# Soft routing over eight experts: five pairs of the first outer product in front, and in four of them a third splitting of inner products 1 and 5

## The chip, the cores and the metric

The kernel runs on one core of one Trainium2 chip. Five engines work side by side, each through its own list of instructions and in order: TensorE (PE, matrix multiplies into the eight banks of PSUM), VectorE (DVE), ScalarE (ACT), GpSimd (POOL, which here mostly issues transfers) and SyncE (SP, which issues transfers). Semaphores order them against each other. The metric is the device time in microseconds; smaller is better. What is compared is the median of several runs.

## The reference

```python
logits_max = np.max(router_logits, axis=-1, keepdims=True)
probs = np.exp(router_logits - logits_max)
probs = probs / np.sum(probs, axis=-1, keepdims=True)
for e in range(n_experts):
    expert_out = np.matmul(x, expert_weights[e])
    output += probs[:, :, e:e+1] * expert_out
```

x has 16 x 512 = 8192 rows (tokens) of 512, there are 8 experts with weights of 512 x 2048, and the output has 8192 x 2048. Since the probability of an expert scales a row, the sum over experts is one product: for a token, the eight scaled copies of its row lie side by side (4096 long) and are multiplied by the eight weight matrices stacked on each other (4096 x 2048).

## The kernel before

**Two levels of seven products.** That large product is cut by the method of Strassen in Winograd's form, which makes a 2 x 2 block product out of seven block products and some sums instead of eight. The outer level halves the experts (0 to 3, 4 to 7) and the output columns, and pairs two blocks of 256 tokens. Its seven products have the numbers r = 1 to 7, and each is taken for 16 values of q, one for each pair of token blocks. `product(r, q)` (L615 of the kernel before) sets one up; such a pair (r, q) is called an instance here. An instance multiplies a left operand of 256 tokens by 2048 (four experts of 512) with a right operand of 2048 x 1024.

The inner level cuts an instance again into seven. The left operand has two tiles `t[0]` and `t[1]` (two experts each), every one with eight chunks of 128 in the contraction and 256 tokens. Class `Left` (L426) makes them on VectorE (`times`, x times probability, 128x2048), and makes from them the difference `s2` (128x1024) and the differences `i` (128x2048). The right operands w[1] to w[7] are tiles of eight chunks by 512 columns; some are weight blocks as they were cast, others are differences that VectorE makes (128x4096). One inner product is eight matmuls, each with 128 x 128 stationary values from the left operand and 512 moving columns. So an instance is 7 x 8 matmuls.

**Steps and banks.** The inner products are taken in the order `STEPS = (1, 5, 6, 2, 7, 3, 4)`. `Product.step` (L498) issues the matmuls. Steps 1, 6, 7 and 4 go on accumulating in one PSUM bank x; steps 5 and 3 use a bank q; step 2 adds onto a bank b. `Product.post` (L506) then evacuates the partial sum: for an instance without a base, ScalarE copies x to b after step 1 (L519), copies q and x into SBUF tiles after steps 5 and 6 (L523), copies after steps 2 and 4 (L527), and VectorE adds after steps 7 and 3. For an instance that continues on an earlier result (a base), VectorE adds at nearly all steps (`post_on_base`). Every finished 128x512 piece is sent to HBM by POOL: the first outer product goes to a buffer `kept`, others to the output.

**Pools.** One PSUM pool has eight buffers, which are the eight banks. In SBUF, tag w has 15 buffers (weights, 128x4096), z has 8 (left operands), h has 12 (pieces of 128x512), and d has 3 (`s2`).

**Stages.** `add` collects one or two instances in a stage; there are 15 of them up to r = 5. A stage with two takes the steps of both alternately, 14 slots in all. `run` (L685) goes through the slots; after each it lets VectorE do other work (`slack`) and evacuates. Hooks placed with `at(stage, slot, ...)` start weight casts, fetches of kept pieces and sums at a slot. The first stages are four pairs of r = 1 (q = 2 to 9), then six stages that hold r = 2 for q = 9 to 14 beside r = 1 for q + 1, whose result passes from the one to the other on chip, and then five pairs of r = 2. The weights for r = 2 are cast in stages 0 to 2 and summed in stage 3. `wedge_at` makes weights of later outer products in stages 4 to 9.

**What orders the work.** A planner in the program keeps two clocks, `clock["pe"]` and `clock["dve"]`. Sums for VectorE wait in `queue` with a planned cost. `slack` advances TensorE's clock by one step (`SLOT`, 1.73) and takes tasks from the queue while VectorE's clock is more than `LAG` behind it; `evacuated` charges an evacuation to VectorE. The resulting order is fixed when the kernel is built. Each engine follows it strictly.

**The head.** Instances r = 1, q = 0 and 1 are computed directly, before the stages. TensorE scales x by diagonal matrices (`early_z0`), and then for each half n of the columns adds 64 matmuls of 512 columns into four banks (the loop `for n in range(2)`). After each n ScalarE copies the four banks out (L331). Meanwhile VectorE and ScalarE work out the softmax of all tokens (`softmax_of_all`, casts at L296 and L297), and for n = 1 TensorE also transposes x for the next two instances (`early_xp1`).

In the listing `ps` is any PSUM tile, `mm` (L127 in the rows of the profile) issues a matmul, and `tt` (L107) issues a VectorE operation on two tensors.

Of the kernel before, what the change touches and what calls it, by code (L numbers as in the profile page):

```python
# [31 lines left out]
def kernel(  # L32
# [51 lines left out]
    with tc.tile_pool(name="psum0", bufs=1, space=bass.MemoryType.PSUM) as psum0:  # L84
# [21 lines left out]
    def tt(o, a, b, op):  # L106
        dve(nc.vector.tensor_tensor(out=o, in0=a, in1=b, op=op))  # L107
# [14 lines left out]

    def bank():
        return psum.tile([P, NB], f32, name="ps", tag="ps")

    def mm(ps, z, w, start, stop):
        note(nc.tensor.matmul(ps, z, w, start=start, stop=stop, skip_group_check=True))  # L127
# [3 lines left out]
    def new_w():  # L131
        return wpool.tile([P, K8, NB], f16, name="w", tag="w")
# [31 lines left out]
    def inner_sums(b, t7=None):  # L164

        w = {1: b[0, 0], 2: b[1, 0], 3: b[1, 1], 7: t7 or b[0, 1]}

        def step(p, x, y):
            if p not in w:
                w[p] = new_w()  # L170
            tt(w[p], x, y, SUB)
        return w, {5: lambda: step(5, b[0, 1], b[0, 0]), 6: lambda: step(6, b[1, 1], w[5]),
                   4: lambda: step(4, b[1, 0], w[6]), 7: lambda: step(7, b[1, 1], b[0, 1])}

    def softmax(lg, J, pf):
        mx = h_tile([P, J], f32)
# [71 lines left out]

    def early_z0(e, d):
        for j in range(4):  # L250
            ps = bank()
# [10 lines left out]

    def early_xp1(j, d):
        t, rows = j // 2 - 2, ds(j % 2 * P, P)
        ps = bank()
# [3 lines left out]
        ps = bank()  # L269
# [38 lines left out]
    for n in range(2):  # L308
        ps = [bank() for _ in range(4)]
        for e in range(HE):  # L310
            if n == 0 and e < 2:
                early_z0(e + 2, ds_[e + 2])
                if e == 0:
                    ds_.append(diag_e(3))
            if n == 0 and e == 2:
                ph0.append(early_p(1))
                ds_ = [diag_j(j) for j in range(4, 8)]
                softmax_of_all()
                w, sums = inner_sums(b11, new_w())
            for c in range(C):  # L320
                for j in range(4):
                    mm(ps[j], z0[j][:, e, c], b11[e // 2, n][:, e % 2 * C + c, :],
                       e + c == 0, e == HE - 1 and c == C - 1)
            if n == 1:
                for j in ((4, 5), (6, 7), (), ())[e]:
                    early_xp1(j, ds_[j - 4])
                if e == 1:
                    sums[5]()
        for j in range(4):
            o = half()  # L330
            act(nc.scalar.copy(o, ps[j]))  # L331
            sp(kept[j // 2][n].rearrange("(p j) m -> j p m", j=2)[j % 2], o)
# [31 lines left out]
        (queue.appendleft if first else queue.append)(t)  # L364
        return t

    def slack():
        clock["dve"] = max(clock["dve"], clock["pe"])
        clock["pe"] += SLOT
        while queue and clock["dve"] < clock["pe"] - LAG:  # L370
            queue.popleft().run()

    def evacuated():
        clock["dve"] = max(clock["dve"], clock["pe"]) + 0.69


    x_dram = {}
# [48 lines left out]
    class Left:  # L426
# [36 lines left out]
        def op(self, p):  # L463
# [4 lines left out]
                    3: (self.i, 0), 7: (self.i, 1)}[p]  # L468
            return t[:, :, ds(i * HP, HP)]

    class Right:


# [16 lines left out]
    class Product:  # L490
# [41 lines left out]
        def post_on_base(self, p, x, q, b):  # L532
# [13 lines left out]
            else:  # L546
                tt(o[tn], q if p in (5, 3) else x, base, ADD)


    def out_rows(q, odd, cols, tn):  # L550
        t, n = tn
# [24 lines left out]
    def at(stage, slot, make):  # L576
        hooks.setdefault((stage, slot), []).append(make)
# [37 lines left out]
    def product(r, q, **how):  # L615
        left, loads = left_of(r, q)
        lefts[r, q] = left
        p = None
        if r == 1:
            def sink(tn, o):  # L620
                pool(kept_rows(q)(tn), o)
            p = Product(right[1], left, sink)
        elif r == 2:
            if q >= 9:
# [24 lines left out]
        products[r, q] = p  # L649
        return p  # L650
# [23 lines left out]
    def queue_left(left):  # L674
        if not left.task:
            left.queue_make(0)
            left.queue_s2()
            left.queue_make(1)

    def queue_lefts(stage):  # L680
        if stage < len(stages):
            for p in stages[stage]:
                queue_left(p.left)

    def run(stage):  # L685
        some = stages[stage]
        for p in some:
            p.left.queue_i()
        n = 0
        for i in range(len(some[0].steps)):  # L690
            for p in some:
                for make in hooks.get((stage, n), ()):
                    make()
                p.step(p.steps[i])
                slack()
                p.post(p.steps[i])
                n += 1
                if n == 1:
                    queue_lefts(stage + 1)
                if n == late.get(stage, 1):  # L700
                    start_loads(stage + 2)
                if n == 5:
                    store_loads(stage + 1)
                if n == 7:
                    finish_loads(stage + 2)
# [10 lines left out]
    forget(*range(0, 18, 2))  # L716
    rest = [15] + list(range(9))
    for i in range(0, 10, 2):
        k = add(product(2, rest[i]), product(2, rest[i + 1]))
        for slot, tn in zip((8, 10, 12, 13), INNER):  # L720
            for q in rest[i:i + 2]:
                if q < 9:
# [83 lines left out]
    def cast21(kn):  # L806
        b21[kn] = cast_block(21, kn)

    for i, kn in enumerate(((0, 0), (0, 1), (1, 1), (1, 0))):
        at((11 * i + 8) // 14, (11 * i + 8) % 14, lambda kn=kn: cast21(kn))  # L810

    def sums_at(stage, slot, r, of, ps):
        def go():
            if right[r].w is None:
                right[r].sums = right[r].build(of)
            for p in ps:
                right[r].queue_sum(right[r].sums, p)
        at(stage, slot, go)
    sums_at(3, 3, 2, b21, (5,))
    sums_at(3, 5, 2, b21, (6,))  # L820
    sums_at(3, 7, 2, b21, (7,))
    sums_at(3, 12, 2, b21, (4,))
# [224 lines left out]
```

## Time and profile before

| what | value |
|---|---|
| median of three runs | 1375.59 us (1375.47 to 1375.77) |
| the profiled execution's own time | 1376.63 us |
| its span | 1374.9 us |
| TensorE busy | 1367.3 us, 99% of the span |
| VectorE busy | 1108.6 us, 81% |
| ScalarE busy | 183.1 us, 13% |
| POOL busy | 411.8 us, 30% |
| DMA read and written | 207.65 MB and 156.43 MB in HBM |

The profile is of one execution. Its times start with the span, and what lies around the span is the difference to the execution's own time. A row of instructions names the line, engine, operation and tiles (out<-in), the shapes, the count, the busy time with the mean length of one, and the idle time of the engine before these instructions with what ended it. In the timeline, a row is a start, a length, the engine and its instructions merged. Matmuls overlap in the pipeline: a row's length runs from the first start to the last end, and the mean length of one is longer than the distance between two starts. A line such as L107 or L127 is a helper through which most instructions of that engine go, so tiles and shapes tell them apart.

### The profile page before, as it was taken

The numbers are of one execution on the slowest core, as the hardware profiler recorded it, in microseconds if no ns is written. First come the engines' busy times: TensorE is split into PE (matmuls) and PEld (weight loads), VectorE is DVE, ScalarE is ACT, GpSimd is POOL, SyncE is SP. The second block draws the span as 40 slices with busy tenths as digits, with TensorE's granted clock in tenths as the row PEclk, the third lists the DMA queues.
The fourth block names the chain that finished last, engine by engine and source line by source line (L and its number), as shares of the span: only waits on it lengthen the run. The fifth ranks groups of instructions, "written<-read, shape, count | busy, mean of one in ns | idle before, by whom it ended". The sixth has DMA issues, their size and how long they took to land.

```text
span 1374.9 us, 17480 instructions
## 1 busy us (share of the span) xinstructions
PE 1367.3 (99%) x6390; PEld 622.0 (45%) x6390; DVE 1108.6 (81%) x1290; ACT 183.1 (13%) x317; POOL 411.8 (30%) x652
## 2 busy tenths in 40 slices
PE   8999999999999999999999999999999999999998
PEld 4444444444444444444444444444444444444444
DVE  5846757669889888798897988889889898988882
ACT  3222111100011111111111100000000000222221
POOL 3222333241223342334232122242333322232221
PEclk9999999999999999999999999999999999999999
DMA  9998999999898998899898998988898979987786
GB/s 183 222 261 205 211 248 265 241 299 378 240 323 249 285 300 246 259 261 265 245 276 263 338 392 219 224 236 212 229 237 223 247 204 316 249 187 177 166 150 106
DMA packets 191271, 338.02 MB, mean 246 GB/s; under 512 B 52944, under 2 KB 86992, under 8 KB 187472
## 3 DMA queue, kind: packets, MB, share of 16 engines
q0 software_dynamic: 88688, 185.12, 55.8%
q1 hardware_dynamic: 98464, 123.34, 30.8%
q10 hardware_dynamic: 4032, 28.44, 5.3%
q8 instruction: 50, 0.82, 0.2%
q14 instruction: 37, 0.30, 0.1%
HBM read 207.65 MB, written 156.43 MB: 265 GB/s over the span
## 4 chain that ended last, share of the span: by engine, by line
PE 98%; DMA 2%; POOL 0%; issue 0%; ACT 0%; POOLq 0%
PE ps L127 98%; DMA w<-wd 1%; DMA w<-in_expert_weights_dram 1%; POOL w L121 0%; ACT h L999 0%; POOL ident L211 0%; POOLq L211 0%; POOLq L1031 0%
## 5 line engine op out<-in xcount | busy, mean ns | idle before, releaser
L127 PE MATMUL ps<-w,z 128*128 128x512 f16 x5416 | 1177.3, 379 | 1.3 <-DMA w<-in_expert_weights_dram 1.1
L127 PEld LDWEIGHTS <-z 128*128 128x128 f16 x5416 | 529.7, 98 | 638.6 <-DMA w<-in_expert_weights_dram 1.3
L121 POOL DMA_DIRECT2D out_dram<-h x380 | 248.9, 672 | 746.4 <-ACT h L540 373.7
L107 DVE TENSOR_TENSOR h<-ps,h 128x512 f32<-128x512 f32 x415 | 282.5, 687 | 207.6 <-PE ps L127 192.8
L107 DVE TENSOR_TENSOR z<-xT,pT 128x2048 f16<-128x2048 f16 x220 | 266.8, 1216 | 11.5 <-DMA xT<-xs 6.3
L127 PE MATMUL ps<-w,d 128*128 128x512 f16 x880 | 199.1, 379 | 0.0
L127 PEld LDWEIGHTS <-d 128*128 128x128 f16 x880 | 86.1, 98 | 103.8
L107 DVE TENSOR_TENSOR z<-z,d 128x2048 f16<-128x2048 f16 x110 | 132.1, 1215 | 0.0
L107 DVE TENSOR_TENSOR w<-w 128x1024 f16<-128x1024 f16 (+2 forms) x92 | 100.8, 1102 | 5.1 <-DMA wd<-w 3.4
L527 ACT COPY h<-ps 128x512 f32<-128x512 f32 x90 | 52.8, 586 | 373.4 <-PE ps L127 336.3
L540 ACT COPY h<-ps 128x512 f32<-128x512 f32 x64 | 37.5, 587 | 486.3 <-PE ps L127 459.9
L107 DVE TENSOR_TENSOR d<-z 128x1024 f16<-128x1024 f16 x110 | 75.2, 685 | 6.8 <-PE ps L127 5.0
L107 DVE TENSOR_TENSOR z<-z,u 128x2048 f16<-128x2048 f16 x64 | 78.4, 1225 | 2.2
L107 DVE TENSOR_TENSOR u<-xT,pT 128x2048 f16<-128x2048 f16 x64 | 77.9, 1217 | 0.0
L523 ACT COPY h<-ps 128x512 f32<-128x512 f32 x90 | 52.8, 587 | 173.9 <-PE ps L127 162.5
L121 POOL DMA_DIRECT2D w<-in_expert_weights_dram x65 | 49.0, 785 | 33.8 <-DMA wd<-w 24.0
L121 POOL DMA_DIRECT2D wd<-w x86 | 48.3, 585 | 36.0 <-DVE w L107 26.4
L107 DVE TENSOR_TENSOR ps<-ps,h 128x512 f32<-128x512 f32 (+1 forms) x66 | 45.3, 688 | 13.0 <-PE ps L127 13.0
L121 POOL DMA_DIRECT2D kept<-h x56 | 30.8, 551 | 76.8 <-ACT h L527 48.2
L107 DVE TENSOR_TENSOR h<-h 128x512 f32<-128x512 f32 (+2 forms) x69 | 45.1, 674 | 0.1
L519 ACT COPY ps<-ps 128x512 f32<-128x512 f32 x45 | 25.6, 570 | 114.6 <-PE ps L127 114.6
L107 DVE TENSOR_TENSOR z<-z 128x2048 f16<-128x2048 f16 x32 | 39.2, 1225 | 1.1
(47 smaller groups left out, 97.0 us busy)
## 6 DMA issues: line engine op xcount, KB each, us to landing
out_dram<-h POOLq DMA_DIRECT2D x380, 256.0 KB, 6.2
pT<-p_dram SPq DMA_DIRECT2D x140, 256.0 KB, 6.0
w<-wd ACTq DMA_DIRECT2D x27, 1024.0 KB, 9.9
h<-kept SPq DMA_DIRECT2D x100, 256.0 KB, 5.6
xT<-x SPq DMA_DIRECT2D x87, 256.0 KB, 5.5
wd<-w POOLq DMA_DIRECT2D x72, 256.0 KB, 5.5
w<-in_expert_weights_dram POOLq DMA_DIRECT2D x35, 512.0 KB, 10.1
h<-out_dram SPq DMA_DIRECT2D x68, 256.0 KB, 5.6
```

The source lines that it names most:

```text
L107: dve(nc.vector.tensor_tensor(out=o, in0=a, in1=b, op=op))
L121: note(nc.gpsimd.dma_start(out=o, in_=i, **how))
L127: note(nc.tensor.matmul(ps, z, w, start=start, stop=stop, skip_group_check=True))
L519: act(nc.scalar.copy(self.banks["b"], x))
L523: act(nc.scalar.copy(o[tn], q if p == 5 else x))
L527: act(nc.scalar.copy(o[TN[p]], b if p == 2 else x))
L540: act(nc.scalar.copy(o[tn], b))
```

## The change

The stages in front become five pairs of r = 1 (q = 2 to 11; `QK = 11`), then four stages with r = 2 for q = 11 to 14 beside r = 1 for q + 1, and six pairs of r = 2. The number of stages stays 15. Casts and sums of weights and the wedges move to stages up to one later (`ND = QK // 2`). Instances 9 and 10 of r = 2 now fetch their base from `kept`.

In stages 1 to 4, the inner products 1 and 5 of both instances of the pair are split a third time. The left block matrix of that level has the two instances as its rows and the two halves of `t[0]` (experts) as its columns; the right one is w[1] or w[5], cut into 4 chunks each way by 256 columns. Each of the two products becomes seven short steps of four matmuls with 256 columns. `third_sums` makes the right differences once, in the head, into two more w tiles; class `Thirds` makes four left sums (128x1024) a stage into h tiles. `by_thirds` issues the 14 short steps in a fixed order, with one x bank for each of the products 1 and 5, one q bank shared by both, and four banks g and h that collect the sums, which the rest of the stage then uses as its x and q. Evacuations in between are copies of 256 columns on ScalarE and adds of 256 columns on VectorE.

The PSUM pool is divided: six buffers for tag ps and two for tag pt. The q bank of ordinary stages, the two x banks of `by_thirds`, and every second bank of `early_z0` and `early_xp1` in the head come from pt.

```diff
-    psum = ctx.enter_context(tc.tile_pool(name="psum", bufs=8, space=bass.MemoryType.PSUM))
+    psum = ctx.enter_context(tc.tile_pool(name="psum", bufs=6, space=bass.MemoryType.PSUM))
...
+    def bank2():
+        return psum.tile([P, NB], f32, name="pt", tag="pt", bufs=2)
...
+    def third_sums(w):
+
+        t = new_w().rearrange("p (s c) (h n) -> p s c h n", s=2, h=2)
+        t = {5: t[:, 0, :, 0], 6: t[:, 0, :, 1], 7: t[:, 1, :, 0], 4: t[:, 1, :, 1]}
+        b = w.rearrange("p (k c) (h n) -> p k c h n", k=2, h=2)
+        tt(t[5], b[:, 0, :, 1], b[:, 0, :, 0], SUB)
+        tt(t[6], b[:, 1, :, 1], t[5], SUB)
+        tt(t[7], b[:, 1, :, 1], b[:, 0, :, 1], SUB)
+        tt(t[4], b[:, 1, :, 0], t[6], SUB)
+        return {**t, 1: b[:, 0, :, 0], 2: b[:, 1, :, 0], 3: b[:, 1, :, 1]}
...
                 w, sums = inner_sums(b11, new_w())
+                third = {1: third_sums(w[1])}
...
-                if e == 1:
+                if e == 0:
                     sums[5]()
+                elif e == 1:
+                    third[5] = third_sums(w[5])
...
+    class Thirds:
...
+        def make(self):
+            e0, e1 = ds(0, C), ds(C, C)
+            a, b = self.a.t[0], self.b.t[0]
+            for p, x, y, op in ((5, b[:, e0], b[:, e1], ADD), (6, None, a[:, e0], SUB),
+                                (3, a[:, e1], None, SUB), (7, a[:, e0], b[:, e0], SUB)):
+                o = self.s[p] = h_tile([P, C, HQ], f16)
...
-                self.banks[b] = bank()
+                self.banks[b] = (bank if p == 1 else bank2)()
...
+    def by_thirds(stage):
...
+        for n, (p, r) in enumerate(((1, 1), (5, 1), (1, 5), (1, 6), (5, 6), (5, 5), (1, 2),
+                                    (1, 7), (5, 7), (1, 3), (1, 4), (5, 2), (5, 3), (5, 4))):
...
+            for c in range(C):
+                mm(o, z[:, c, :], w[:, c, :], (r == 1 or (p, r) == (1, 5)) and c == 0, c == C - 1)
+            slack(0.4375, LAG if n < 6 else 1.3)
+            if r == 1:
+                act(nc.scalar.copy(g[:, cols[0]], x))
+            elif r == 5:
+                act(nc.scalar.copy(keep[p][:, cols[1]], q))
+            elif r == 6:
+                act(nc.scalar.copy(keep[p][:, cols[0]], x))
+            elif r == 7:
+                evacuated(0.42)
+                tt(at_once(("h", p))[:, cols[1]], x, keep[p][:, cols[1]], ADD)
+            elif r == 3:
+                evacuated(0.42)
+                tt(g[:, cols[1]], q, keep[p][:, cols[0]], ADD)
...
+            elif r == 4:
+                act(nc.scalar.copy(place["h", p][:, cols[0]], x))
...
-    for q in (2, 4, 6, 8):
+    for q in range(2, QK, 2):
         add(product(1, q), product(1, q + 1))
-    for q in range(9, 15):
+    for q in range(QK, 15):
         add(product(2, q), product(1, q + 1))
...
-    rest = [15] + list(range(9))
-    for i in range(0, 10, 2):
+    rest = [15] + list(range(QK))
+    for i in range(0, QK + 1, 2):
         k = add(product(2, rest[i]), product(2, rest[i + 1]))
...
-        at((11 * i + 8) // 14, (11 * i + 8) % 14, lambda kn=kn: cast21(kn))
+        at((14 * i + 8) // 14, (14 * i + 8) % 14, lambda kn=kn: cast21(kn))
...
-        wedge_at(4 + i, 2, kn, e, (4 + i, 11))
+        wedge_at(ND + i, 2, kn, e, (ND + i, 11))
...
+    for stage in range(1, ND):
+        thirds[stage] = Thirds(*(p.left for p in stages[stage]))
```

A short step is written (p, r) below: p is the inner product that is split, 1 or 5, and r is which of its seven it is.

More of the change, by code (lines that the diff above doesn't have):

```diff
@@ L250, in early_z0 @@
         for j in range(4):
-            ps = bank()
+            ps = (bank, bank2)[j % 2]()
             for c in range(C):
@@ L264, in early_xp1 @@
         t, rows = j // 2 - 2, ds(j % 2 * P, P)
-        ps = bank()
+        ps = (bank, bank2)[j % 2]()
         for c in range(C):
@@ L268, in early_xp1 @@
         evacuate(xp1[t][0][:, :, rows], ps.rearrange("p (c t) -> p c t", c=C), 0)
-        ps = bank()
+        ps = (bank, bank2)[j % 2]()
         mm(ps, ones, d.rearrange("p e t -> p (e t)"), True, True)
@@ L365, in later, with slack, evacuated @@
         return t
-    def slack():
+    def slack(slot=SLOT, lag=LAG):
         clock["dve"] = max(clock["dve"], clock["pe"])
-        clock["pe"] += SLOT
-        while queue and clock["dve"] < clock["pe"] - LAG:
+        clock["pe"] += slot
+        while queue and clock["dve"] < clock["pe"] - lag:
             queue.popleft().run()
-    def evacuated():
-        clock["dve"] = max(clock["dve"], clock["pe"]) + 0.69
+    def evacuated(cost=0.69):
+        clock["dve"] = max(clock["dve"], clock["pe"]) + cost
     x_dram = {}
@@ L469, in op, with __init__, queue @@
             return t[:, :, ds(i * HP, HP)]
+    class Thirds:
+        def __init__(self, a, b):
+            self.a, self.b, self.s, self.task = a, b, {}, None
+        def make(self):
[4 more added lines that the diff above has]
+                o = self.s[p] = h_tile([P, C, HQ], f16)
+                x = self.s[5] if x is None else x
+                y = self.s[6] if y is None else y
+                tt(o, x, y, op)
+        def queue(self):
+            self.a.queue_make(0)
+            self.b.queue_make(0)
+            self.task = later(2.76, self.make)
+            for left in (self.a, self.b):
+                left.queue_s2()
+            for left in (self.a, self.b):
+                left.queue_make(1)
+        def op(self, p, part):
+            need(self.task)
+            a, b = self.a.t[0], self.b.t[0]
+            z = {1: a[:, 0:C], 2: a[:, C:K8], 4: b[:, C:K8]}.get(p)
+            return (self.s[p] if z is None else z)[:, :, ds(part * HP, HP)]
     class Right:
@@ L547, in post_on_base @@
                 tt(o[tn], q if p in (5, 3) else x, base, ADD)
+    QK = 11
+    ND = QK // 2
     def out_rows(q, odd, cols, tn):
@@ L623, in product @@
         elif r == 2:
-            if q >= 9:
+            if q >= QK:
                 base = products[1, q].o.__getitem__
@@ L678, in queue_left, with at_once @@
             left.queue_make(1)
+    thirds = {}
+    def by_thirds(stage):
+        some = stages[stage]
+        left = thirds[stage]
+        cols = [ds(i * HQ, HQ) for i in range(2)]
+        place, keep = {}, {}
+        def at_once(what):
+            if what not in place:
+                t = place[what] = (bank2 if what[0] == "x" else bank)()
+                if what[0] in "gh":
+                    some["gh".index(what[0])].banks["x" if what[1] == 1 else "q"] = t
+            return place[what]
+        slot = 0
+        for n, (p, r) in enumerate(((1, 1), (5, 1), (1, 5), (1, 6), (5, 6), (5, 5), (1, 2),
+                                    (1, 7), (5, 7), (1, 3), (1, 4), (5, 2), (5, 3), (5, 4))):
+            if n in (0, 4, 7, 11):
+                for make in hooks.get((stage, slot), ()):
+                    make()
+                slot += 1
+                if slot == 2:
+                    queue_lefts(stage + 1)
+                    start_loads(stage + 2)
+            x = at_once(("x", p))[:, cols[0]]
+            q = at_once("q")[:, cols[p // 5]] if n > 1 else None
+            g = at_once(("g", p))
+            if r == 1:
+                keep[p] = half()
+            o = q if r in (5, 3) else g[:, cols[0]] if r == 2 else x
+            z, w = left.op(r, p // 5), third[p][r]
+            for c in range(C):
+                mm(o, z[:, c, :], w[:, c, :], (r == 1 or (p, r) == (1, 5)) and c == 0, c == C - 1)
+            slack(0.4375, LAG if n < 6 else 1.3)
+            if r == 1:
+                act(nc.scalar.copy(g[:, cols[0]], x))
[9 more added lines that the diff above has]
+                tt(g[:, cols[1]], q, keep[p][:, cols[0]], ADD)
+                if p == 1:
+                    some[0].post(1)
+            elif r == 4:
+                act(nc.scalar.copy(place["h", p][:, cols[0]], x))
+                if p == 1:
+                    some[1].post(1)
+        for product in some:
+            product.post(5)
+        return 4
@@ L680, in queue_lefts @@
     def queue_lefts(stage):
-        if stage < len(stages):
+        if stage in thirds:
+            if thirds[stage].task is None:
+                thirds[stage].queue()
+        elif stage < len(stages):
             for p in stages[stage]:
@@ L688, in run @@
             p.left.queue_i()
-        n = 0
-        for i in range(len(some[0].steps)):
+        n = by_thirds(stage) if stage in thirds else 0
+        for i in range(n // 2, len(some[0].steps)):
             for p in some:
@@ L709, in fetch_at @@
             at(stage, slot, lambda tn=tn: base.fetch(tn))
-    for q in (2, 4, 6, 8):
+    for q in range(2, QK, 2):
         add(product(1, q), product(1, q + 1))
-    for q in range(9, 15):
+    for q in range(QK, 15):
         add(product(2, q), product(1, q + 1))
-    forget(*range(0, 18, 2))
-    rest = [15] + list(range(9))
-    for i in range(0, 10, 2):
+    forget(*range(0, 2 * QK, 2))
+    rest = [15] + list(range(QK))
+    for i in range(0, QK + 1, 2):
         k = add(product(2, rest[i]), product(2, rest[i + 1]))
@@ L721 @@
             for q in rest[i:i + 2]:
-                if q < 9:
+                if q < QK:
                     fetch_at(k if tn == (1, 0) else k - 1, 3 if tn == (1, 0) else slot, bases[2, q], tn)
@@ L818, in sums_at @@
         at(stage, slot, go)
[L819 to L822, printed above, removed]
+    sums_at(ND - 1, 3, 2, b21, (5,))
+    sums_at(ND - 1, 5, 2, b21, (6,))
+    sums_at(ND - 1, 7, 2, b21, (7,))
+    sums_at(ND - 1, 12, 2, b21, (4,))
     for i, (kn, e) in enumerate((kn, e) for kn in ((0, 0), (1, 0), (1, 1)) for e in range(2)):
-        wedge_at(4 + i, 2, kn, e, (4 + i, 11))
+        wedge_at(ND + i, 2, kn, e, (ND + i, 11))
     def fetch_at_w(stage, slot, of, what, kn):
```

## The prediction

> **What bounds the kernel now.** I read the page's first two parts, then the chain, then TensorE's rows by shape, and last the stretches that the change touches.
>
> ```profile
> PE 1367.3 (99%) x6390; PEld 622.0 (45%) x6390; DVE 1108.6 (81%) x1290; ACT 183.1 (13%) x317; POOL 411.8 (30%) x652
> ...
> PEclk9999999999999999999999999999999999999999
> ```
>
> TensorE is busy 99% of the span, and the granted clock is full in every slice. A busy PE is not yet a streaming PE, so the chain, in order of time:
>
> ```profile
> 10.75 775.35 PE ps L127 x3616
> 786.10 14.93 DMA w<-wd
> 801.07 570.07 PE ps L127 x2648
> ```
>
> From 10.75 us on the chain is the matmul stream and one fetch of weights. Its rows by shape, with the two vector engines' rows for 256 columns:
>
> ```profile
> L127 PE MATMUL ps<-w,z 128*128 128x512 f16 x5400 | 1175.6, 379 | 1.3 <-DMA w<-in_expert_weights_dram 1.1
> L127 PE MATMUL ps<-w,d 128*128 128x512 f16 x880 | 199.1, 379 | 0.0
> ...
> L127 PE MATMUL ps<-w,z 128*128 128x256 f16 x16 | 2.1, 272 | 0.0
> ...
> L127 PEld LDWEIGHTS <-z 128*128 128x128 f16 x5416 | 529.7, 98 | 638.6 <-DMA w<-in_expert_weights_dram 1.3 <-DMA w<-wd 0.6
> ...
> L999 ACT COPY h<-ps 128x256 f32<-128x256 f32 x1 | 0.4, 372 | 11.5 <-PE ps L127 11.5
> ...
> L107 DVE TENSOR_TENSOR ps<-ps,h 128x256 f32<-128x256 f32 x2 | 0.8, 428 | 3.3 <-PE ps L127 3.3
> ```
>
> 379 and 272 ns are lengths of overlapping matmuls, not what one costs. The cost is the distance between starts, and the timeline has it:
>
> ```profile
> 25.25 3.83 PE L127 MATMUL ps<-w,z 128*128 128x512 f16 x17
> ...
> 28.92 0.39 PE L127 MATMUL ps<-ident,w 128*128 128x128 f16 x4
> 29.14 0.38 PE L127 MATMUL ps<-h,ones 128*128 128x512 f16 x1
> ...
> 1369.88 1.25 PE L127 MATMUL ps<-w,z 128*128 128x512 f16 x9
> ```
>
> 17 matmuls of 512 columns: (3.83 - 0.379) / 16 = 0.2157 us each. Four of 128 columns start within 0.22 us: 0.055 each. The last line is one of 512 and the kernel's last eight of 256: (1.25 - 0.216 - 0.272) / 7 = 0.109 each. From 10.75 us, 6284 x 0.2157 + 16 x 0.109 + 32 x 0.055 = 1359 us of the 1360.4 that are left: the rest is rounding, a hole of 0.3 us at 801 and the last matmul's drain. The kernel is as long as its matmul columns, and a microsecond of new waiting anywhere is a microsecond of time.
>
> **The change, part by part.**
>
> *Columns.* In each of four stages, steps 1 and 5 of two products are 32 matmuls of 512 columns; they become 14 short steps of 4 matmuls of 256. Over the four stages 128 x 0.2157 = 27.61 us go and 224 x 0.109 = 24.42 come: **-3.19 us**. The 16 matmuls at the kernel's end are the same shape, each with its own weights. All of it is on the path.
>
> *The head, with six banks where there were eight.* This is the part the words of the change do not mention. The loop over n keeps four accumulators. For n = 1 it asks for four more banks at once, and of the six in that pool only two are free; the other two are accumulators of n = 0 that ScalarE has yet to copy out. In the built order the third matmul of n = 1 waits for the first of those copies and the fourth for the second; before, all four had idle banks. ScalarE then:
>
> ```profile
> 25.44 0.62 ACT L296 CAST h<-h 128x512 f16<-128x512 f32 x1 [3.37 <-DVE h L107]
> 25.97 0.40 ACT L297 CAST h<-h 128x256 f16<-128x256 f32 x1
> 26.28 2.04 ACT L331 COPY h<-ps 128x512 f32<-128x512 f32 x4
> ```
>
> It is busy with two casts of the softmax, so the first copy starts at 26.28 and ends at 26.87, the second, 0.48 later, at 27.35. The last matmul of n = 0 starts at 25.25, so n = 1 begins at 25.47 and its third matmul is due at 25.90. I take 0.05 for a release: in the last product the rows leave one hole of 0.07 us, where the matmul starts 0.05 after the add that it waits for. Third matmul at 26.92 (1.02 late), fourth due 27.14 and at 27.40 (0.26): **+1.28 us**. The bounds are 0, if ScalarE were free by then, and 1.28 plus a copy, 0.48. I take 1.28, since nothing in the change moves the softmax that feeds the casts. The later banks of the head come free earlier than TensorE, now later, asks for them.
>
> *VectorE in the head.* Eight sums of 128x1024 (the 685 ns row, 0.61 from start to start) are new. Four follow the softmax, which ends at 25.6, and end near 28.2; VectorE waited until 29.34 there, for TensorE's transposes. The sum for step 5 comes earlier, and four more stand ahead of the first left operands. Those are ready near 40.1, against a first stage that begins at 41.04 before and 42.3 now. Cost 0; without that cover up to 4 x 0.61 = 2.4 us.
>
> *Inside a split stage.* Count from its start; a step is 4 x 0.109 = 0.437 us. An evacuation starts 0.20 after its step's slot ends (at the kernel's end 1371.17 against 1370.97). The built order has five waits that matter, and with 0.37 a copy and 0.43 an add I get: (1,6) is due at 1.31 and needs the copy of (1,1), which stands behind the last copy of the stage before and ends at 1.07; (5,6), due 1.75, copy ends 1.45; (5,5), due 2.18, ends 1.88; (1,4), due 4.37, add of (1,7) ends 4.13; (5,3), due 5.24, add of (1,3) ends 5.00. After the release 0.19 to 0.25 us are spare at each. Cost 0. From above, a wait could miss by what a 512-column copy (570 ns) exceeds the 372, some 0.2 less the spare, so about 0.1: 20 waits, 2 us.
>
> *VectorE, ScalarE and h tiles there.* Per stage VectorE gets four sums (2.5 us) and four short adds (1.7), ScalarE eight short copies (3.0). VectorE had 12.6 and 11.3 us of work in the second and third stage of 24.2. What counts is whether it is idle when the add of (1,7) is due at 3.70. Ahead of it stand the two 1.2 us differences of the stage. They follow the adds of step 3, which end 2.6 us before the stage begins, so they end at -0.2; in the first split stage, behind the rest of the next operands, at about 2.4. Cost 0. Four sum tiles and two held tiles a stage come out of the same 12 h buffers. The tightest is a sum tile wanted near 8.5 whose buffer was stored from near -2.6; kept blocks land 7.8 us after issue (median, 40 to 90 us), so it is free at 5.2.
>
> *Queues.* SP gets eight fetches of kept blocks and two of x (instances 9 and 10 are no longer joined on chip), 2.6 MB on 338: fractions of a microsecond for the engines, and nobody waits for it. POOL has the same number of transfers; weight blocks and wedges start up to a stage later, still stages ahead of their readers. From there on TensorE's order is that of before. Cost 0, at most the 0.3 us hole that the 801.07 line already holds.
>
> **Sum.** -3.19 + 1.28 = -1.91 us. The profiled execution took 1376.63 (span 1374.9), 1.04 over the median; on the median that is 1375.59 - 1.9 = **1373.7 us**, 0.14% faster. A measurement of this kernel tells about 0.2% (2.75 us) from no change, so this is "the same".
>
> **The rivals.**
>
> *The head does not wait.* If ScalarE's copies come before the casts or the scheduler's banks are free after all, the whole -3.19 stays: 1372.4, just beyond 0.2%. Against it stands the row at 26.28. Below 0.44 us of waiting this case decides. 12%.
>
> *The five waits miss.* Slower release than 0.05, or short copies near the 512 price: up to 0.1 at each of 20 places, 1 to 2 us: 1374.7 to 1375.7. The spare is thin, but rows for both short shapes give it. 13%.
>
> *VectorE is late in the split stages (slower).* VectorE runs in order. If h buffers or x transposes hold it so that the two 1.2 us differences are still ahead of it at 3.70, TensorE stands at (1,4): up to 2.4 - 0.2 = 2.2 us a stage, 8.8 in four, 1382.5. It takes 1.16 us in each of four stages (4.64 in all) to be slower by 0.2%, so VectorE would have to run some 3 us behind the walk in the first and 5 in the others. For it: a wait of 5.30 us for a transpose stood on VectorE at 75.03. Against: its slack is nearly half of each stage. 13%.
>
> *The weight loads show (slower).* A load takes 98 ns by its row and a 256-column matmul 109; if the load could not run beside the matmul before it, each would cost 207 and four stages 224 x 0.098 = 22 us more, 1395.7. It decides from 0.123 us a matmul against the bare gain. The 128-column matmuls, which start 55 ns apart although each loads for 98, speak against it, and so do the last eight. 3%. [...]
>
> **How the numbers follow.** Forecast 59%, within 0.2%; the missed waits 13%, also within; no head wait 12%, faster; the two slower ones 16%. So faster 0.12, same 0.72, slower 0.16. The range goes from the whole gain, 1372.3, to missed waits with the head's extra copy of 0.48 on top, 1376.2; it leaves out the 16%. The likeliest case alone is 1373.2 to 1374.4.
>
> **What would show it.** Starts of 256-column matmuls 0.109 apart in four stretches of 6.1 us; a split stage of 23.4 us against 24.2; two holes of about 1.0 and 0.3 us at 25.9 to 27.4, TensorE waiting for the line of the accumulators' copy; no PE wait on a short copy or add. I am wrong if the head shows no hole, if the split stretches are longer than 6.3 us, or if a hole appears after them.

## The result: 0.45% slower, and where the time came from

| | before | after |
|---|---|---|
| median | 1375.70 us (six runs, 1375.47 to 1376.85) | 1381.99 us (six runs, 1380.69 to 1383.15) |
| profiled execution, own time | 1376.63 us | 1380.69 us |
| its span | 1374.9 us | 1379.0 us |
| TensorE busy | 1367.3 us | 1367.6 us |

The ratio is 1.0045 (95% interval 1.0032 to 1.0058): about 6.2 us slower, where 1.9 us faster was forecast. The profiled execution is the fastest of the six, so it shows less of the loss than the median has: 4.1 us of span.

**What came out as planned.** The timeline of TensorE in the second split stage, after the change (start, length, instructions merged, the count behind x, and in brackets the idle time before them):

```profile
89.15 1.04 PE L130 MATMUL pt<-w,z 128*128 128x256 f16 x8
...
95.26 2.11 PE L130 MATMUL ps<-w,d 128*128 128x512 f16 x9
```

The 56 short matmuls of the stage take 95.26 - 89.15 = 6.11 us, 0.109 each, and no row has a bracket: no short step waits. The other three split stages look the same. The -3.19 us of columns are there.

In the head, the same view:

```profile
19.81 5.99 PE L130 MATMUL ps<-w,z 128*128 128x512 f16 x27
26.19 3.45 PE L130 MATMUL ps<-w,z 128*128 128x512 f16 x14 [0.39 <-ACT h L348]
```

TensorE waits for ScalarE's copies of the accumulators (now L348), as forecast. From start to start it loses 0.55 us before the third matmul of n = 1 and 0.27 before the fourth, 0.82 in all.

**What was not foreseen.** TensorE's timeline from 325 us on, more than 150 us after the last split stage:

```profile
325.77 7.07 PE L130 MATMUL ps<-w,z 128*128 128x512 f16 x32 [0.46 <-DVE h L107]
...
339.28 1.89 PE L130 MATMUL ps<-w,d 128*128 128x512 f16 x8 [1.26 <-DVE ps L107]
341.00 3.62 PE L130 MATMUL ps<-w,z 128*128 128x512 f16 x16
347.83 5.23 PE L130 MATMUL ps<-w,z 128*128 128x512 f16 x16 [3.21 <-DVE h L107]
```

Each bracket is a hole. Start to start they are 0.62, 1.43 and 3.38 us; two small ones, 0.03 and 0.08, stand before them. Behind the last, 16 matmuls take 5.23 us where 16 at 341.00 take 3.62: the first eight run at half speed (granted clock 0.50 from 347.73 to 351.14 us), 1.6 us more. Together 7.1 us. Before the change TensorE has no hole of 0.1 us or more between 15 and 800 us.

The balance of the two spans: -3.19 columns, +0.82 in the head for banks, -0.25 for the rest of the head (earlier waits for weights, other in each execution), -0.3 since the hole at 801 is absent, -0.1 behind the last matmul, +7.1 here: +4.1, as measured. Nearly everything that was lost was lost in stages 11 and 12, where neither a short matmul nor a third split exists.

**What the holes wait for.** The chain of waits of the changed kernel, cut to the stretch 280 to 362 us (start, length, what):

```profile
300.80 18.46 DMA w<-in_expert_weights_dram
...
319.81 0.40 POOL out_dram L121
...
320.70 11.27 DMA out_dram<-h
...
332.02 14.94 DMA h<-kept
...
347.09 0.70 DVE h L107
...
347.83 5.23 PE ps L130 x16
```

Read from below: TensorE at 347.83 needs a PSUM bank that VectorE empties at 347.09; that addition needs a kept block, which took 14.94 us to land; SP could only ask for it at 332.02, when a store had left an h tile; that store took 11.27 us and was issued late by POOL, which by this chain had been held by a weight cast that took 18.46 us. TensorE's own rows say VectorE, VectorE's rows say transfer:

```profile
303.92 1.23 DVE L107 TENSOR_TENSOR u<-w 128x2048 f16<-128x2048 f16 x1 [3.88 <-DMA w<-in_expert_weights_dram]
```
```profile
338.53 0.70 DVE L107 TENSOR_TENSOR ps<-ps,h 128x512 f32<-128x512 f32 x1 [2.55 <-DMA h<-kept]
343.34 0.69 DVE L107 TENSOR_TENSOR h<-pt,h 128x512 f32<-128x512 f32 x1 [4.11 <-DMA h<-kept]
```

The transfers of the stretch 286 to 334 us, by kind (kind, queue, count, KB each, median us from issue to landing), before:

```profile
out_dram<-h POOLq DMA_DIRECT2D x16, 256.0 KB, 11.6
h<-kept SPq DMA_DIRECT2D x12, 256.0 KB, 5.8
...
w<-in_expert_weights_dram POOLq DMA_DIRECT2D x4, 512.0 KB, 11.0
```

and after:

```profile
out_dram<-h POOLq DMA_DIRECT2D x17, 256.0 KB, 14.3
h<-kept SPq DMA_DIRECT2D x14, 256.0 KB, 8.4
w<-in_expert_weights_dram POOLq DMA_DIRECT2D x6, 512.0 KB, 16.0
```

Six casts instead of four, two fetches more, and these three kinds land later by 2.6 to 5.0 us. The two casts are the sixth wedge: wedges moved one stage later, so the sixth stands in stage 10, where the casts of the odd weights 11 and 22 already stood and stand unmoved. The pairs of r = 2 with fetched bases begin one stage earlier, at stage 9. Both moves bring load towards the same 60 us. At the end of it, from 320 to 340 us, the busy share of the DMA engines in 40 slices, before and then after:

```profile
DMA  9998999699999979999999999999999999999999
...
DMA packets 2065, 7.71 MB, mean 385 GB/s; under 512 B 268, under 2 KB 268, under 8 KB 1553
```
```profile
DMA  9999999999999999999999999999999999999999
...
DMA packets 2491, 8.38 MB, mean 419 GB/s; under 512 B 321, under 2 KB 321, under 8 KB 2084
```

Before, the engines have slices that are not full, 385 GB/s on the mean: the transfers have caught up. After, no slice has room at 419 GB/s: a backlog is still being worked off, and in it stand the fetches that VectorE waits for at 338 and 343.

### The profile page after: what moved, and what is told of

It reads as the page before. It is cut to its first block, busy times and chain, and to the rows that moved or that the text cites. A ratio compares the mean times of both kernels' runs of the same rounds, so it can differ in the third digit from the quotient of the medians.

```text
span 1379.0 us, 17763 instructions
## 1 busy us (share of the span) xinstructions
PE 1367.6 (99%) x6486; PEld 632.3 (46%) x6486; DVE 1128.9 (82%) x1330; ACT 192.8 (14%) x349; POOL 411.6 (30%) x652
## 4 chain that ended last, share of the span: by engine, by line
PE 94%; DMA 5%; DVE 1%; issue 0%; ACT 0%; POOL 0%; DVEq 0%; POOLq 0%; SPq 0%
PE ps L130 68%; PE pt L130 25%; DMA w<-in_expert_weights_dram 3%; DMA h<-kept 1%; DMA out_dram<-h 1%; DVE h L107 0%; POOL w L121 0%; DVE z L107 0%; DVE z L255 0%; ACT h L348 0%; DVE h L195 0%; DVE h L191 0%; DVE h L196 0%; DVE d L107 0%; ACT h L193 0%
## 5 line engine op out<-in xcount | busy, mean ns | idle before, releaser
L130 PE MATMUL ps<-w,z 128*128 128x512 f16 x3688 | 812.7, 378 | 4.9 <-DVE h L107 3.7
L130 PE MATMUL pt<-w,z 128*128 128x512 f16 (+1 forms) x1696 | 378.2, 375 | 0.0
L107 DVE TENSOR_TENSOR h<-ps,h 128x512 f32<-128x512 f32 x248 | 168.6, 688 | 113.7 <-PE ps L130 107.6
L107 DVE TENSOR_TENSOR h<-pt,h 128x512 f32<-128x512 f32 x167 | 114.1, 688 | 66.1 <-PE pt L130 58.8
L107 DVE TENSOR_TENSOR w<-w 128x1024 f16<-128x1024 f16 (+2 forms) x100 | 106.1, 1069 | 5.5 <-DMA wd<-w 3.7
L588 ACT COPY h<-ps 128x512 f32<-128x512 f32 x64 | 37.5, 586 | 514.1 <-PE ps L130 486.8
L575 ACT COPY h<-ps 128x512 f32<-128x512 f32 x90 | 52.8, 586 | 361.0 <-PE ps L130 303.2
L107 DVE TENSOR_TENSOR ps<-ps,h 128x512 f32<-128x512 f32 (+1 forms) x74 | 48.8, 661 | 17.7 <-PE ps L130 15.1
L571 ACT COPY h<-ps 128x512 f32<-128x512 f32 x53 | 30.6, 591 | 80.8 <-PE ps L130 74.2
## 6 DMA issues: line engine op xcount, KB each, us to landing
w<-in_expert_weights_dram POOLq DMA_DIRECT2D x35, 512.0 KB, 11.6
```

Source lines behind the costliest of these rows:

```text
L571: act(nc.scalar.copy(o[tn], q if p == 5 else x))
L575: act(nc.scalar.copy(o[TN[p]], b if p == 2 else x))
L588: act(nc.scalar.copy(o[tn], b))
```

## The experiments

Three theories could make this picture. A: the order of stages, by what the sixth wedge does in stage 10; in one form VectorE is held by the late cast and the sums of the wedge (narrow A), in another the transfers are more than the DMA engines carry (A2). B: six pairs with fetched bases are too much by themselves. C: the split, or the divided PSUM pool, starves something. Each time is given with the ratio to the kernel before that ran beside it; 0.1% is 1.4 us.

| run | edit to the changed kernel (unless said) | median us | ratio, 95% |
|---|---|---|---|
| e1_order | kernel before with the new order alone | 1384.64 | 1.0061 (1.0046 to 1.0076) |
| e2_split | split with the old order | 1375.69 | 0.9996 (0.9987 to 1.0006) |
| e7_nosum | sixth wedge without its sums | 1382.45 | 1.0041 (1.0027 to 1.0055) |
| e8_nocast | sixth wedge without its casts | 1375.94 | 0.9997 (0.9988 to 1.0007) |
| e11_nofetch | two instances' bases not fetched | 1375.60 | 0.9999 (0.9990 to 1.0008) |
| e3_wedge_early | sixth wedge 10 slots earlier | 1379.91 | 1.0026 (1.0015 to 1.0037) |
| e5_odd_late | odd casts half a stage later | 1385.98 | 1.0073 (1.0058 to 1.0088) |
| e12_hpool | 13 h buffers, 9 x buffers | 1382.64 | 1.0044 (1.0030 to 1.0057) |
| e13_sp_out | stores of r = 2 on SP | 1384.49 | 1.0064 (1.0050 to 1.0077) |
| e4_head | head's banks | 1381.97 | 1.0048 (1.0031 to 1.0065) |
| e6_both | head's banks and wedge early | 1378.63 | 1.0017 (1.0007 to 1.0027) |
| e10_split_head | e2_split and head's banks | 1373.73 | 0.9985 (0.9975 to 0.9994) |

### The order alone, and the split alone

The order alone is the kernel before with the lines of the change on stages, bases, casts, sums and wedges (`QK = 11`, `ND = 5`); the split alone is the changed kernel with:

```diff
-    QK = 11
+    QK = 9
...
-        at((14 * i + 8) // 14, (14 * i + 8) % 14, lambda kn=kn: cast21(kn))
+        at((11 * i + 8) // 14, (11 * i + 8) % 14, lambda kn=kn: cast21(kn))
```

> The kernel before with only the new order of stages (five pairs of r = 1 in front, casts, sums and wedges up to a stage later, the base of instances 9 and 10 fetched); no split, eight PSUM banks in one pool. Theory A (the order: the sixth wedge now falls in stage 10 together with casts of odd weights, its sums hold VectorE): the late stall of 7 to 8.4 us is there without the split, 1382.5 to 1384 us, with TensorE waiting for VectorE between 320 and 360 us. Theory B (six pairs with fetched bases are too much by themselves): the same time, so this run does not tell A from B. Theory C (the split or the divided PSUM pool makes the stall): 1375.3 to 1375.9 us and no hole there.

> The split and the divided PSUM pool with the old order of stages: four pairs in front, three of them split, wedges in stages 4 to 9 as before. Theories A and B: 3 x 0.80 = 2.4 us of columns go and the head's 0.8 us of waiting comes, 1374.0 us (1373.5 to 1374.5), no hole after 100 us beyond the 0.3 at 801. Theory C: the stall stays, 1381 us or more.

The order alone is 0.61% slower and has the stall, larger: TensorE's timeline of it shows

```profile
350.94 7.26 PE L127 MATMUL ps<-w,z 128*128 128x512 f16 x24 [5.25 <-DVE h L107]
```

The split with the old order has no hole of 0.1 us or more behind the head. C has fallen: neither the split nor the divided PSUM pool makes the stall. Its median is above what was expected, though: the ratio says about 0.5 us gained, with an interval that holds both nothing and the 1.6 expected. The difference of the two ratios 1.0061 and 1.0045 is 0.16%, 2.2 us: as an estimate what the split gives within the new order, though the two intervals overlap. The forecast's sum for it was -1.91.

### Which part of the wedge

```diff
+        def raw():
+            for what, u in (("t3", b), ("t1", a), ("t2", b)):
+                send(what, u)
+        if (kn, e) == ((1, 1), 1):
+            return casts, [raw]
```

> The changed kernel, but the wedge in stage 10 does no sums: its two casts run as before and POOL sends the casts themselves in place of the three sums (so a part of the weights of later outer products is not what it should be). Same bytes moved, 3.7 us less on VectorE and no wait of VectorE for the cast. Theory A in its narrow form (VectorE is held by the late cast and has no time to catch up): the stall goes, 1373 to 1374.5 us. Theory A2 (it is the transfers that collide): the stall stays nearly whole, 1380 us or more. Theory B: stays, 1380 us or more.

```diff
+        last_one = (kn, e) == ((1, 1), 1)
+        if last_one:
+            a0 = b0 = b21[1, 1][:, rows, :]
         def casts():
+            if last_one:
+                return
```

(The sums then read a0 and b0 in place of the cast blocks.)

> The changed kernel, but the wedge in stage 10 casts nothing: its sums read weights that lie in SBUF already (so a part of the weights of later outer products is not what it should be). VectorE's work stays, 2 MB less is read from HBM in the stage and VectorE waits for no cast there. Theories A and A2: the stall goes, 1373 to 1374.5 us (if it goes in this run and not in the run without the sums, the transfers are the cause; if in both, the wait on VectorE for a late transfer). If it stays here and goes without the sums, VectorE's 3.7 us of work are the cause. Theory B: stays, 1380 us or more.

Without the sums VectorE has no wait for the cast in stage 10 and 3.7 us less to do, and the stall is nearly as it was, 6.7 us in the profile. Its last large hole:

```profile
349.11 3.62 PE L130 MATMUL ps<-w,z 128*128 128x512 f16 x16 [2.51 <-DVE h L107]
```

Without the casts it is gone but for one hole of 0.58 us at 349. (Between 800 and 830 us, where a fetched weight is awaited, the profiles have holes of 0 to 3.8 us, 0.3 before and 1.5 here; they differ from one profile to the next and are left out of the comparison.) The row at 303.92, where VectorE waits 3.88 us for the cast, looked like the start of it all and is not: without that wait the ratio is 1.0041 beside 1.0045. Narrow A has fallen, and A2 is left, the transfers. (The median without the casts comes back to that of the kernel before, not below it to the 1373 to 1374.5 us that were expected.)

### Any two megabytes?

```diff
+            if any(self is bases.get((2, q)) for q in (3, 4)):
+                act(nc.scalar.copy(self.t[tn], right[2].w[1][:, 0, :]))
+            else:
+                sp(self.t[tn], self.source(tn))
```

> The changed kernel, but the bases of instances r = 2, q = 3 and 4 (stage 11) are not fetched: ScalarE fills their eight h tiles from a weight tile in SBUF, so these two instances' rows of the output are not what they should be. 2 MB less are read between 290 and 315 us, as many as the sixth wedge's casts read. If any 2 MB in the stretch do (the sum of the transfers is the cause), the stall goes as it did without the casts: 1375 to 1377.5 us. If it is the casts or the wedge itself, it stays: 1380 us or more.

This leaves the wedge and all casts, and takes away eight fetches of 256 KB. The median falls by as much as without the casts, from +0.45% to -0.01%. Not all of the stall goes: the profiled execution, which is 1.3 us above this run's median, has holes of 2.1 us at 342 and 0.6 at 351. So the wedge is not special. Its two casts write 512 KB each, but read twice that; 2 MB of reading less, of either kind, nearly does it. B in its plain form has fallen as well, since six pairs with fetched bases run without the stall once the sixth wedge reads nothing. That fits the sum of the transfers. Two other readings have to be weighed. The order of issue on one engine could be the cause, but the run without casts changes POOL's list and leaves SP's fetches, this one takes fetches from SP and leaves POOL's list (POOL still waits 3.62 us for a cast at 301.79), and the stall goes in both. And this run also removes fetches that VectorE waits for itself (1.81 us at 317.43 in the changed kernel), so a part of its gain can be the missing wait and not the missing bytes; how much stays open.

### Moving load instead of removing it

```diff
-        wedge_at(ND + i, 2, kn, e, (ND + i, 11))
+        wedge_at(ND + i - i // 5, 2 + i // 5 * 4, kn, e, (ND + i, 11 - i // 5 * 9))
```

> The changed kernel with its sixth wedge some 10 slots earlier: casts in stage 9, slot 6, and sums in stage 10, slot 2. The same work and the same bytes, but the wedge's 2 MB are read in the stretch 261 to 285 us, where the DMA engines were busy 0.96, and stage 10 then has only the odd casts, as in the kernel before. Theory A2 (the transfers of 286 to 345 us are more than the DMA engines carry, because the sixth wedge was put there): the late stall goes, 0 to 1 us is left, 1374.5 to 1376.5 us on a chip where before takes 1376.4. Theory B (six pairs with fetched bases): the stall stays, 1380 us or more.

```diff
-    for stage, slot, q in ((9, 9, 12), (10, 2, 11), (10, 9, 22), (last2, 8, 21)):
+    for stage, slot, q in ((9, 9, 12), (10, 9, 11), (11, 2, 22), (last2, 8, 21)):
...
-    at(11, 6, odd_t)
+    at(11, 11, odd_t)
```

> The changed kernel with the casts of odd weights 11 and 22 about half a stage later (stage 10 slot 9 and stage 11 slot 2) and their sums 5 slots later. No more four casts within 2 us, but all the same bytes within 286 to 345 us. If what matters is that the casts are issued in one cluster, the stall goes: 1374.5 to 1376.5 us. If it is the sum of the bytes in the stretch (A2), it stays or is worse, 1380 us or more.

The wedge 10 slots earlier takes away 2.6 of the 6.2 us, less than I expected, and its 1379.91 us lie close to the 1380 of theory B: where the wedge stands is a part of it, and the six pairs with their fetches fill the stretch too. The windows (busy time by engine, then the granted clock, the DMA engines' share and the rate) of the changed kernel and then of this run:

```profile
261.00:285.00 24.00, 24.00 (x113) 10.92 (x112) 18.42 (x23) 1.17 (x2) 6.46 (x11) 1.00 0.96 241
```
```profile
261.00:285.00 24.00, 24.00 (x113) 10.92 (x112) 18.83 (x23) 1.17 (x2) 7.75 (x13) 1.00 1.16 261
```

A share of 0.96 had looked like room for a wedge; with it the stretch is at 1.16, and the two stretches after it are at 1.10 and 1.05. (The share adds up the times of all packets that start in the window; at 1.16 of the 16 engines' time, some of them must overlap.) But a share above 1 is not yet a stall. The kernel before, in the same stretch and the two after it:

```profile
261.00:285.00 24.00, 24.00 (x113) 10.88 (x112) 16.55 (x20) 3.50 (x6) 8.06 (x14) 1.00 1.10 262
285.00:309.00 24.00, 24.00 (x113) 10.90 (x112) 15.73 (x21) 1.17 (x2) 8.55 (x14) 1.00 1.14 286
309.00:333.00 24.00, 24.00 (x113) 10.84 (x111) 22.05 (x23) 1.18 (x2) 4.87 (x9) 1.00 1.02 365
```

It has no hole there, and is at 0.90 in the 24 us that follow.

The odd casts later are worse still, a hole of 9.0 us at 337, but this run does not answer its question. The casts moved by 7 slots and their sums by 5, and VectorE came to stand before a sum that reads the moved cast itself:

```profile
342.42 2.29 DVE L107 TENSOR_TENSOR w<-w 128x4096 f16<-128x4096 f16 x1 [13.21 <-DMA out_dram<-h]
```

The view names a store, but the second half of the cast of weight 22 was issued at 317.20 and took 25.1 us, to 342.3. TensorE's hole is this wait of VectorE, one that the edit made. Whether a cluster of four casts within 2 us hurts stays open.

### What passes the lateness on

> The changed kernel with 13 h buffers in place of 12, for which x gets 9 in place of 10; every engine's order is the same. A stage of the r = 2 pairs uses eight h tiles in 24.2 us, so one buffer is 3 us of delay. If late stores and fetches reach TensorE through the h tiles, the stall shrinks by up to 3 us, to 1379 to 1381 us. If the missing h tile is not what links them, or the missing x buffer costs as much: 1382 us or more.

> The changed kernel with the stores of r = 2 to the output issued by SP, not by POOL. If it is POOL's own queue that is full (82% of the packets' time between 286 and 334 us) or POOL's waits before issuing that make stores late, the stall shrinks to 0 to 3 us: 1375 to 1378 us. If the 16 DMA engines as a whole are full, the time stays at 1381 to 1384 us, or is longer because SP's fetches then stand behind stores.

The edits are `bufs=13` for h with `bufs=9` for x, and `sp(out_rows(q, 0, 0, tn), o)` as the sink of r = 2. One more h tile leaves the time as it was, but not the stall: in this run's profile it is 4.6 us (a hole of 3.0 at 343 and eight matmuls at half speed, with a granted clock of 0.93 on the mean from 333 to 357 us) instead of 7.1. That is 2.5 us less, within the up to 3 expected of one buffer, and agrees with the chain, which goes from a store to a fetch through an h tile. In return two holes of together 3.6 us stand between 812 and 825 us; whether the x tile that paid for the h tile makes them stays open. Stores on SP are no better, although POOL then issues far less. Of this run's transfers between 286 and 334 us, and then between 280 and 334 us, where all six casts are in the window:

```profile
out_dram<-h SPq DMA_DIRECT2D x12, 256.0 KB, 11.8
```
```profile
w<-in_expert_weights_dram POOLq DMA_DIRECT2D x6, 512.0 KB, 26.2
```

From issue to landing the stores take less (11.8 us for 14.3) and the casts more (26.2 for 16.0). The casts are not that much later: with no stores in its list POOL issues them earlier, from 281.71 to 287.20 us instead of 289.52 to 300.80, and the last lands at 322.8 instead of 319.3. They wait behind their issue instead of on POOL before it. So the stall needs neither POOL's stores nor POOL's waits before them. That POOL has no part in the changed kernel's stall is not shown, because here SP's fetches stand behind stores and land later too (11.4 us for 8.4).

### The head, and the best version

```diff
-        ps = [bank() for _ in range(4)]
+        ps = [(bank2 if n == 1 and j > 1 else bank)() for j in range(4)]
```

with `bank()` alone in `early_xp1`.

> The changed kernel with another choice of banks in the head alone: the third and fourth accumulator of n = 1 come from the pool of two, which is idle there, and the transposes use the pool of six. The holes at 25.4 and 26.2 us go, 0.8 to 1.3 us; the late stall stays: 1380.7 to 1381.7 us against 1382 to 1382.5 for the changed kernel.

> The changed kernel with both: the sixth wedge early and the head's banks chosen as in the run of the head alone. If A2 and the head's term add up: 3.19 us of columns are left as gain, 1373.2 us (1372.7 to 1375) on a chip where before takes 1376.4. Theory B: 1379 us or more.

> The split with the old order of stages (three split stages) and the head's banks chosen so that no accumulator of n = 1 waits. If the split is worth 0.80 us a stage and the head 1.28, 2.4 us are gained: 1373.9 us where before takes 1376.3 (ratio 0.9983), 0.8 to 1.3 us under the run without the head's edit. If the head's gain is swallowed by transfers as in the run of the head alone, it stays at ratio 0.9996.

The holes at 25.4 and 26.2 us are gone from all three profiles. In the changed kernel that shows no gain: 1.0048 beside 1.0045, with intervals of 0.3% in which 0.8 us would not stand out. Whether the backlog swallowed it, as TensorE now comes earlier to the same transfers, stays open. Wedge and head together are at 1.0017, 1378.63 us: between the theories' 1373.2 and 1379, and much nearer to the second. With the old order the edit takes 0.9996 to 0.9985, 1.5 us, where 0.8 to 1.3 was expected, though the two intervals overlap; the whole is as forecast (0.9983). **This version is 0.15% faster than the kernel before and 0.6% faster than the changed one**: three split stages, four pairs in front, no wait in the head. In its chain of waits TensorE has 99% of the span and DMA 1%, against 94% and 5% in the changed kernel.

## Why the prediction was wrong

- *Columns, -3.19.* Right. The short matmuls start 0.109 us apart in all four stages.
- *The head, +1.28.* Right as a mechanism: third and fourth matmul, ScalarE's copies, six banks. The size varies: 0.82 us in the changed kernel's profile, where TensorE had lost 0.5 us for weights at 17.6 and came later to the copies, and 0.92 to 1.93 in those of the eight experiments with this head, 1.28 in three of them. The upper bound, 1.76, was a little low.
- *VectorE in the head, cost 0; the five tight waits, cost 0; VectorE, ScalarE and h tiles in a split stage, cost 0.* Right. No hole of 0.1 us or more between 27 and 317 us in the changed kernel's profile. (Of the experiments' profiles one, with the odd casts later, has a hole in a split stage, 0.43 us at 109, behind the short steps.)
- *The sum, -1.9.* The forecast's two terms stand in the timeline, as -3.19 and +0.82, but no run measures their sum clear of the noise: 2.2 us lie between the ratios without and with the split in the new order, where the intervals overlap, and 0.5 us are gained with the old order, where the interval holds 0. Only with the head's wait taken out is the gain clear, 2.1 us with three split stages.
- *Queues, cost 0.* **This is the step that failed.** It costed eight fetches on SP and the moved casts by the time that the issuing engines spend (0.32 us for a fetch of `kept` on SP, in the median), and said that weight blocks and wedges, a stage later, are still stages ahead of their readers. That is true of the weights, and they are not what was late. It never asked what else the DMA engines carry in the stage into which the sixth wedge moves. The kernel before had a warning: in the windows its DMA share is 1.10 from 261 to 285 us, 1.14 from 285 to 309, where the odd casts stand, and still 1.02 from 309 to 333; room (0.90) comes only after that. What the runs showed in place of the 0 is 7.1 us of stall in stages 11 and 12, where VectorE waits for late fetches; without the wedge's two casts the time is back at that of the kernel before. A step that adds 2 MB there should have been bounded from above by the time those megabytes take. An estimate from the after rows: at 419 GB/s, the rate of the full engines, 2 MB of reading are 5 us; the holes of the profile sum to 7.1.
- *"From there on TensorE's order is that of before."* Also true, and no protection. The same order on TensorE, with other transfers beside it, lost 7 us.
- *The rivals.* The slower one, VectorE late in the split stages, gave 1382.5 us, close to the measured 1382.0, and is still wrong: it would have put its holes into the four split stages, which have none. The rival of the weight loads, which needed 0.207 us a matmul, stays excluded by starts 0.109 us apart.
- *What would make it wrong.* "A hole appears after them" was on the list, and that is what happened. It had no price and no chance of its own among the rivals.

## What to carry to other kernels

When a change shifts the time at which weights are cast or kept pieces are fetched, add up the transfers of every stage that it shifts them into, and read the DMA share of those stages in the profile of before: where it is near 1 and stays there, what is added can make unrelated stores and fetches late (here 14.3 us from issue to landing for 11.6, and 8.4 for 5.8), however early its own data is there. The share is a warning and not a measure: the kernel before ran at 1.10, 1.14 and 1.02 without a hole, and the stretch at 0.96 did not take a wedge for nothing. A load that is "stages ahead of its reader" can cost time through other loads that are not (here a ratio of 1.0045 with the sixth wedge's casts and 0.9997 without). And a wait in the trace (here VectorE's 3.88 us for a cast) is a suspect only until a run without it loses as much, and a run that moves a load is to be looked at for waits that the move made.

## What the runs showed of the hardware

- A cast took about as long as a plain transfer of the bytes that it reads, twice those that the profile counts for it (512 KB). The changed kernel's rate from 286 to 334 us, in slices of 1.2 us, with the DMA engines busy 90% or more in all of them:

```profile
DMA  9999999999999999999999999999999999999999
GB/s 318 413 406 423 406 335 405 294 288 258 281 207 286 219 207 205 206 247 373 189 219 217 208 237 338 364 398 406 413 416 406 418 401 408 408 411 444 411 437 430
```

While the casts from float32 to half that width are moved (the six are issued from 289.52 us on, and the last lands at 319.3), slices go down to 189 to 207 GB/s; the plain transfers behind them reach 410. The engines are busy 90% or more in the one as in the other, so the low rate here is no sign of room. The packets say the same: in the packed trace of the kernel before, a cast's packet of 1024 bytes takes 98 ns in the median, while one of a plain transfer takes 46 to 48 ns with 1024 bytes and 84 with 2048, and one of 4096 bytes in POOL's own queue 159. As an estimate from these, the 1024 packets of two casts (1 MB written, 2 MB read) are 6.3 us of the 16 engines, and the 1024 packets of eight fetches (2 MB) 5.4 us; in the experiments they weighed about the same (1375.94 us without the casts, 1375.60 without the fetches).
- A hole can cost more than its length, and the length alone does not decide it. In the changed kernel the 3.21 us before 347.83 were followed by eight matmuls at half speed (16 in 5.23 us). With 13 h buffers 2.78 us were enough for that (16 in 5.30 us); with the wedge early, 3.36 us before 346.27 were not (16 in 3.62 us, and a granted clock of 1.00 from 333 to 357 us). The windows of the half speed, 3.41 us long, and of as much before it in the changed kernel, and then two of that length around the hole with the wedge early (the second number is the time with matmuls, the third from the end the granted clock):

```profile
344.31:347.73 3.42, 0.31 (x2) 0.03 (x1) 2.79 (x5) 0.58 (x1) 0.62 (x2) 1.00 1.05 411
347.73:351.14 3.41, 3.31 (x8) 1.13 (x8) 3.38 (x5) 0.00 (x0) 0.00 (x0) 0.50 1.00 332
```
```profile
341.32:344.74 3.42, 1.59 (x8) 0.60 (x7) 1.62 (x3) 1.11 (x2) 1.08 (x2) 1.00 1.02 397
344.74:348.15 3.41, 1.88 (x9) 0.87 (x9) 3.41 (x5) 0.00 (x0) 0.00 (x0) 1.00 1.00 296
```

In the first pair 3.11 us of one window are without a matmul, and the next is at half speed. In the second pair the longer hole lies in both windows, with 1.83 and 1.53 us of them, and the clock stays at 1.00. That it matters how a hole is spread is my reading of these two profiles; no run tests it.
